# Two-layer trunk, first mixer: a fourth raw weight tile, memory's keys loaded behind head 0, Silus and exponentials pinned, the last output weights split first

## The chip, the cores and the metric

One Trainium2 chip; the kernel runs on one of its cores. The metric is the device time of one execution in microseconds (us), as the median of several runs. The engines are named as in the profile: PE (TensorE, matrix products; PEld are its weight loads), DVE (VectorE), ACT (ScalarE), POOL (GpSimd) and SP (SyncE, which issues most DMAs). POOL issues DMAs too. Each engine works through its own instructions in a fixed order; a letter q behind its name (SPq, POOLq) means its queue of issued DMAs and waits.

## The reference

An encoder trunk of two layers over 512 positions of width 1024, in float32. Each layer has a mixer and a gated channel mixer, both with a residual. The change lies in the first layer's mixer:

```python
h = rmsnorm(x, norm_mix_g[l])
proj = h @ a_w_in[a]
qk, v, o, gates, q_mem = jnp.split(proj, [...], axis=-1)
qk = jax.nn.silu(causal_dwconv(qk, a_conv_w[a], a_conv_b[a]))
q, k = jnp.split(qk, 2, axis=-1)
ig, fg = jnp.split(gates + a_gate_b[a], 2, axis=-1)
hm = mlstm_chunkwise(q, k, v, ig, log_sigmoid(fg))      # 4 heads of 192
hm = hm * lax.rsqrt(jnp.mean(hm * hm, axis=-1) + EPS) * a_head_g[a]
mix_out = hm * jax.nn.sigmoid(o)
mem_out = memory_attention(q_mem, mem, mem_w_kv[l])     # 4 heads of 64 over 256 tokens
x = x + jnp.concatenate([mix_out, mem_out], axis=-1) @ w_out
x = x + conv_ffn(rmsnorm(x, norm_ffn_g[l]), ...)
```

The second layer has a band attention of 12 heads in the place of the matrix memory (mLSTM), the same memory attention over its own keys and values, and the same form of output projection and channel mixer.

## The kernel before

**Products in three parts.** Activations stand as transposed tiles of 128 channels by 512 positions. Each float32 operand is split into a high part, rounded to the fp32r type (a cast on ACT, L130), and a low part, the difference (a subtraction on DVE, L131). A product is three matmuls: high by high, high by low, low by high (`mm3`, L169 to L171). A projection of 128 output channels (`project`) loads a weight tile of 128 x 1024 (`load`, L143, into a raw tile `wr`), splits it into `wh` and `wl` (`parts`), and runs eight `mm3`, 24 matmuls of 512 columns, into one PSUM bank.

**Pools.** Tiles with one tag share a fixed number of buffers (`bufs`): raw weights `wr` 3, their halves `wh` and `wl` 3 each, general tiles `u` 57, small tiles `s` 16, rows `bias` 4. An instruction that writes a tile waits until a buffer of its tag is free.

**The order of the instructions.** In the mixers a compile-time scheduler orders each engine's instructions: at each simulated moment it takes, of those that are ready, the one that was traced first. So the order in which the Python program traces is a priority, not a fixed order. `pin` (keep in program order) adds one edge: the instruction comes behind the one that was traced just before it on the same engine. The channel mixers' main loop has a fixed order written out by hand.

**The first mixer**, from about 60 to 262 us of the profile. `value_columns` makes the values; `gate_rows` turns the gates into rows `exponents` in DRAM and, at its end, columns `acol` and `floor2` (an Exp, L1099). `a_tiles` makes, for tile j, queries and keys (`qk_tile(j)`, `qk_tile(6 + j)`: projection, an Identity with the first conv tap on ACT (L1108), three taps on DVE (L1111), a Silu (L1112), then splits) and the output gate (`o_tile`, a Tanh, L1126). Tiles 3hp + 1 are shared by two heads: their halves go to masked tiles (`head_queries`, L499 to L503; `head_keys`, L509, L510).

A head (`mlstm_head`) goes through four steps s of 128 keys (`weighted_scores`): an Exp of a row of exponents (L1155), the issue of a later row's load, a causal mask on POOL (`affine_select`, L1157), the score matmuls into PSUM (`psc`), their product with the Exp on DVE (L1166), and a split into `pt` (L130, L131). The products with the values follow (`ptr`), then squares (L1193), statistics (L1200, L1201), a chain of small DVE instructions, a spread over the partitions (L244), and the split of the result into `mixes`. `spread_exponents` (L1029) loads a row of exponents, broadcast over the partitions, into a `bias` tile; `NEXT` (4) rows are loaded ahead, counted over all heads in order, so that the 16 rows are issued as the Exp four places before them is through.

`memory_attention` computes scores (L519), a softmax (L573 to L579, its Exps L576), transposes (L588), products (L602) and `values` (L538, L539). Its keys and values for both layers were computed at the start and spilled to DRAM; `load_memory_kv` (L523) loads them and splits them again (L509, L510, L130, L131).

`weave(job, filler, each)` advances the projections of the filler by a number of steps (one `mm3` each) for each step of a head or an attention. At the end the filler is the output projection: `OutProjection.part` adds up five of the eight output columns while heads are still at work, and `finish` computes the last three, adds the residual (L633), spills x (L634) and prepares the channel mixer's input. `finish` and `memory_attention` serve the second layer too, whose bands also use `bias` tiles.

The order of the stages around the change:

```python
weave(chain(value_columns(0), a_tiles(0, 1)), fill, 0.3)
run(fill)
fill = chain(a_tiles(2), a_memory_queries(0), a_tiles(3, 4), a_tiles(5), a_memory_queries(1))
memkv = load_memory_kv(0)
weave(mlstm_head(0), fill, 1.4)
until(lambda: og[2] is not None, fill)
weave(mlstm_head(1), fill, 1.125)
until(lambda: memq[0] is not None, fill)
weave(memory_attention(memq[0], memkv, 0, mixes), fill, 1.463, 4)
...
```

Of the kernel before, what the change touches and what calls it, by code (L numbers as in the profile page):

```python
# [12 lines left out]
AF = mybir.ActivationFunctionType  # L13
# [3 lines left out]
P = 128  # L17
D = 1024
S = 512
KT = D // P  # L20
TT = S // P
# [34 lines left out]
def trunk(  # L56
# [19 lines left out]
    V, A, G = nc.vector, nc.scalar, nc.gpsimd  # L76
# [2 lines left out]
    pool = ctx.enter_context(tc.tile_pool(name="pool", bufs=1))  # L79
    psum = ctx.enter_context(tc.tile_pool(name="psum", bufs=1, space=bass.MemoryType.PSUM))  # L80

    bufs = {"wr": 3, "wh": 3, "wl": 3, "u": 57, "t": 8, "pt": 2, "s": 16, "rb": 3, "bias": 4}
    pbufs = {"mm": 3, "sc": 3, "tr": 2}
    count = [0]
    dram = ctx.enter_context(tc.tile_pool(name="dram", bufs=1, space=bass.MemoryType.DRAM))
# [41 lines left out]
    pin = tc.keep_in_program_order  # L127
# [32 lines left out]
    def weights(*args):  # L160
        return parts(load(*args))

    def rows(w, c0, n, k0=0, k1=None):
        k1 = k1 if k1 is not None else w.shape[0] // P
        return w[k0 * P : k1 * P, c0 : c0 + n].rearrange("(k p) c -> p k c", p=P)
# [4 lines left out]
        nc.tensor.matmul(o, lh, rl, start=False, stop=False, skip_group_check=more)  # L170
        nc.tensor.matmul(o, ll, rh, start=False, stop=last, skip_group_check=more)  # L171

    def project(w, c0, act, tag="mm"):


        n = len(act)
        wh, wl = weights(rows(w, c0, P), n, P)
        o = ps(tag)
        for k in range(n):
            mm3(o, wh[:, k, :], wl[:, k, :], act[k][0], act[k][1], k == 0, k == n - 1)  # L180
            yield
        return o

    def run(gen):
        while True:
            try:
                next(gen)
            except StopIteration as end:
                return end.value

    def chain(*gens):
        for g in gens:
            yield from g
# [15 lines left out]
    def until(there, filler):  # L209
        while not there():  # L210
            next(filler)
# [35 lines left out]
    def logarithms():  # L247

        pin(A.preload_act_table_set("natural_log_exp_and_others"))
# [128 lines left out]
    ss = small(2 * TT).rearrange("p (c t) -> p c t", c=2)  # L378
# [43 lines left out]
    with tc.manual_schedule(engines={mybir.EngineType.PE, mybir.EngineType.Activation, mybir.EngineType.DVE}):  # L422

        w = ps("mm")
# [96 lines left out]
    def load_memory_kv(l):  # L521
        raw = sb("wr", [P, D])
        nc.sync.dma_start(raw, spill[l])  # L523
        k = head_keys(raw[:, :S])
        vs = []
        for m in range(2):
            v = sb("u", [P, S], F32R).rearrange("p (h c) -> p h c", h=4)
            src = raw[:, S + m * MEM : S + (m + 1) * MEM].rearrange("p (h c) -> p h c", h=4)
            split(v[:, :, :HD], v[:, :, HD:], src)
            vs.append(v)  # L530
        return k, vs
# [25 lines left out]
    def memory_attention(q, kv, hp, mixes):  # L557

        k, vs = kv
        pts = [sb("pt", [P, 5 * S], F32R) for _ in range(2)]  # L560
        pth = [p[:, : 2 * S].rearrange("p (a t) -> p a t", a=2) for p in pts]
        ptl = [p[:, 2 * S : 4 * S].rearrange("p (a t) -> p a t", a=2) for p in pts]
        es = {}

        def softmax(T2):
            ss = [ps("sc").rearrange("p (t m) -> p t m", t=2) for _ in range(2)]
            for i in range(2):
                T = 2 * T2 + i
                scores([s[:, i, :] for s in ss], q, slice(T * P, (T + 1) * P), k, slice(hp * MEM, (hp + 1) * MEM))
                yield  # L570
            for h in range(2):
                mx, sm = small(2), small(2)
                V.tensor_reduce(mx, ss[h], axis=AX.X, op=ALU.max, negate=True)  # L573
                e = sb("t", [P, S]).rearrange("p (t m) -> p t m", t=2)
                for i in range(2):
                    A.activation(e[:, i, :], ss[h][:, i, :], AF.Exp, bias=mx[:, i : i + 1], accum_out=sm[:, i : i + 1])  # L576
                V.reciprocal(sm, sm)
                for i in range(2):
                    V.tensor_scalar(e[:, i, :], e[:, i, :], sm[:, i : i + 1], None, op0=ALU.mult)  # L579
                es[T2, h] = e  # L580
                yield

        def transposed(T2):
            for h in range(2):
                tp = ps("tr").rearrange("p (a t c) -> p a t c", a=2, t=2)
                for i in range(2):
                    for a in range(2):
                        nc.tensor.transpose(tp[:, a, i, :], es[T2, h][:, i, a * P : (a + 1) * P], ident)  # L588
                tsl = slice(2 * T2 * P, 2 * (T2 + 1) * P)
                split(pth[h][:, :, tsl], ptl[h][:, :, tsl], tp.rearrange("p a t c -> p a (t c)"))  # L590
                yield

        yield from softmax(0)
        yield from softmax(1)
        yield from transposed(0)
        yield from transposed(1)
        outs = []
        for h in range(2):
            o2 = ps("tr")
            outs.append(o2)  # L600
            for i, (a, p) in enumerate(((0, pth), (0, ptl), (1, pth), (1, ptl))):
                nc.tensor.matmul(o2, vs[a][:, 2 * hp + h, :], p[h][:, a, :], start=i == 0, stop=i == 3)  # L602
            yield
        mixes[6 + hp] = values(outs)
        yield

    class OutProjection:
# [18 lines left out]

        def finish(self, gnames):
            logarithms()
            norm = Norm()
            acts = [[] for _ in gnames]  # L630
            for j in range(KT):
                o = self.o[j] if j in self.o else run(project(self.w, j * P, self.mixes))
                V.tensor_add(xT[j], xT[j], o)  # L633
                pin(G.dma_start(xspill[j], xT[j]))  # L634
                norm.add(xT[j])
                for a, g in zip(acts, gnames):
                    a.append(scaled(xT[j], g[:, j : j + 1]))
            return norm, acts
# [374 lines left out]
    tot = cpool.tile([AH, 16], F32, name="tot")  # L1013
    acol = cpool.tile([P, TT, AH], F32, name="acol")
    floor2 = cpool.tile([P, TT, AH], F32, name="floor2")
    NEXT = 4
    RO = [0, 512, 896, 1152, 1280]

    exponents = dram.tile([TT, AH, S], F32, name="exponents")
# [11 lines left out]
    def gate_rows():  # L1031
# [64 lines left out]
            nc.tensor.transpose(tp[:, T * AH : (T + 1) * AH], ar[:, T * P : (T + 1) * P], ident[:AH, :AH])  # L1096
            nc.tensor.transpose(tp[:, 16 + T * AH : 16 + (T + 1) * AH], mr[:, T * P : (T + 1) * P], ident[:AH, :AH])
        pin(V.tensor_copy(acol, tp[:, :16].rearrange("p (t h) -> p t h", t=TT)))
        A.activation(floor2, tp[:, 16:32].rearrange("p (t h) -> p t h", t=TT), AF.Exp, scale=-2.0)  # L1099

    mixes = [None] * KT

    def qk_tile(c):

        o = yield from project(w_in, c * P, act)
        acc = sb("t", [P, S])
        cw, cb = col["cw"], col["cb"]
        A.activation(acc, o, AF.Identity, scale=cw[:, 36 + c : 37 + c], bias=cb[:, c : c + 1])  # L1108
        for i in (1, 2, 3):
            w = cw[:, 12 * (3 - i) + c : 12 * (3 - i) + c + 1]  # L1110
            V.scalar_tensor_tensor(acc[:, i:], o[:, : S - i], w, acc[:, i:], op0=ALU.mult, op1=ALU.add)  # L1111
        A.activation(acc, acc, AF.Silu)  # L1112
        if c % 3 == 1:
            return (head_queries if c < 6 else head_keys)(acc)
        hi, lo = sb("u", [P, S], F32R), sb("u", [P, S], F32R)
        split(hi, lo, acc)
        return hi, lo
# [14 lines left out]
    def a_tiles(*js):  # L1132
        for j in js:
            qs[j] = yield from qk_tile(j)
            ks[j] = yield from qk_tile(6 + j)
        for j in js:
            og[j] = yield from o_tile(j)
# [3 lines left out]
    def a_memory_queries(hp):  # L1141
        memq[hp] = queries((yield from project(w_in, 4 * AW + 2 * AH + hp * P, act)), None)

    def mlstm_head(h):
# [6 lines left out]
        def weighted_scores(s):  # L1151
            n = S - s * P
            sl = slice(s * P, (s + 1) * P)
            e = sb("t", [P, S])
            A.activation(e[:, :n], spreads.pop((h, s)), AF.Exp, bias=acol[:, s, h : h + 1])  # L1155
            spread_exponents(order.index((h, s)) + NEXT)
            G.affine_select(  # L1157
                out=e[:, :P], in_=e[:, :P], pattern=[[1, P]], base=0, channel_multiplier=-1,
                compare_op=ALU.is_ge, fill=0.0,
            )  # L1160
            yield
            o = ps("sc")
            kf, qf = ks[full], qs[full]
            mm3(o[:, :n], kf[0][:, sl], kf[1][:, sl], qf[0][:, s * P :], qf[1][:, s * P :], True, False)
            head_scores(o[:, :n], odd, qs[sh], slice(s * P, S), ks[sh], sl, False, True)
            V.scalar_tensor_tensor(e[:, :n], o[:, :n], DH**-0.5, e[:, :n], op0=ALU.mult, op1=ALU.mult)  # L1166
            split(pt[:, RO[s] : RO[s + 1]], pt[:, 1280 + RO[s] : 1280 + RO[s + 1]], e[:, :n])
            yield
# [54 lines left out]
    fill = gate_rows()  # L1223
    weave(chain(value_columns(0), a_tiles(0, 1)), fill, 0.3)
    run(fill)
    fill = chain(a_tiles(2), a_memory_queries(0), a_tiles(3, 4), a_tiles(5), a_memory_queries(1))
    memkv = load_memory_kv(0)
    weave(mlstm_head(0), fill, 1.4)
    until(lambda: og[2] is not None, fill)
    weave(mlstm_head(1), fill, 1.125)  # L1230
    until(lambda: memq[0] is not None, fill)
    weave(memory_attention(memq[0], memkv, 0, mixes), fill, 1.463, 4)
# [290 lines left out]
```

## Time and profile before

| | |
|---|---|
| runs shown | 1194.70, 1194.93, 1196.32 us; median 1194.93 |
| the profiled execution | 1195.72 us; its span 1194.0 us |
| granted TensorE clock | 0.999 |
| instructions | 18184 |
| HBM | 128.89 MB read, 32.46 MB written, 135 GB/s over the span |

The span runs from the first to the last instruction of the profiled execution; times in the views are microseconds from its start. In a view of groups, the busy time, the mean duration of one instruction in ns and the idle time of the engine before them follow the name. In a timeline stand start, duration, engine, line, operation, tiles written and read, shape and count; in square brackets how long the engine was idle before, and what ended it. In the view of waits stand the waiting engine and tile, what released it, the sum in us, the count and the longest. Neighbouring instructions overlap by some tenths of a microsecond, since the ends are those of the pipeline; for TensorE the distance from start to start tells more than the busy time.

### The profile page before, as it was taken

To read this page: it belongs to the slowest core of one execution; us is meant where nothing else is said; L and a number is where in the kernel's file an instruction comes from. 1 tells how busy PE (TensorE), PEld (TensorE's weight loads), DVE (VectorE), ACT (ScalarE), POOL (GpSimd) and SP (SyncE) were. 2 spreads that over 40 slices of the span, in tenths; PEclk is the share of its full clock that TensorE was granted. 3 is DMA by queue.
4 is the path that set the end of the run, shared out by engine and by line. 5 is a ranking of instruction groups with operands and counts; after the bars stand their busy time and mean duration, and the time that the engine had idled before them with its cause. 6 is when DMAs were issued, how large, how long until landed. Compare 5 with 4: busy or idle time off the path is not lost.

```text
span 1194.0 us, 18184 instructions
## 1 busy us (share of the span) xinstructions
PE 1183.5 (99%) x6719; PEld 1037.0 (87%) x6719; DVE 961.7 (81%) x1760; ACT 725.2 (61%) x1294; POOL 130.3 (11%) x222
## 2 busy tenths in 40 slices
PE   9999999999999999999999999999999999999997
PEld 9988888888899998999888888888889988999986
DVE  6877788788978888888698888997896888888855
ACT  5648677655656555555576677776565655555545
POOL 1211201010021111111020000101001011011100
PEclk9999999999999999999999999999999999999999
DMA  8645313444265676665464313246336455665551
GB/s 289 212 108 140 84 54 80 152 144 141 88 156 147 156 165 165 154 144 123 142 204 123 89 54 101 69 135 185 111 99 141 116 139 135 142 141 139 119 158 71
DMA packets 200155, 158.61 MB, mean 133 GB/s; under 512 B 8344, under 2 KB 179838, under 8 KB 200066
## 3 DMA queue, kind: packets, MB, share of 16 engines
q1 hardware_dynamic: 183906, 119.74, 34.1%
q0 software_dynamic: 15584, 36.67, 14.9%
q8 instruction: 53, 0.87, 0.3%
q10 hardware_dynamic: 576, 1.05, 0.2%
q14 instruction: 36, 0.29, 0.1%
HBM read 128.89 MB, written 32.46 MB: 135 GB/s over the span
## 4 chain that ended last, share of the span: by engine, by line
PE 92%; ACT 3%; DVE 2%; DMA 1%; SPq 1%; issue 0%; POOL 0%; POOLq 0%; DVEq 0%; ACTq 0%
PE pmm L169 15%; PE pmm L170 15%; PE pmm L171 15%; PE ptr L171 6%; PE ptr L169 6%; PE ptr L170 6%; PE pmm L785 6%; PE psc L171 5%; PE psc L170 5%; PE psc L169 5%; PE pmm L784 3%; PE psc L519 2%; PE ptr L1350 1%; DMA wr<-in_mem_w_kv_dram 1%; PE ptr L1371 1%; PE ptr L1372 1%
## 5 line engine op out<-in xcount | busy, mean ns | idle before, releaser
L169 PE MATMUL pmm<-u,wh 128*128 128x512 f32 (+1 forms) x872 | 309.1, 355 | 0.3 <-ACT u L130 0.2
L170 PE MATMUL pmm<-u,wh 128*128 128x512 f32 (+1 forms) x872 | 306.2, 351 | 0.0
L171 PE MATMUL pmm<-u,wl 128*128 128x512 f32 (+1 forms) x872 | 306.0, 351 | 0.0
L131 DVE TENSOR_TENSOR wl<-wr,wh 128x1024 fp32r<-128x1024 f32 (+3 forms) x172 | 199.8, 1163 | 57.0 <-ACT wh L130 55.0
L130 ACT CAST wh<-wr 128x1024 fp32r<-128x1024 f32 (+3 forms) x172 | 172.4, 1004 | 97.7 <-PE pmm L170 44.5
L171 PEld LDWEIGHTS pmm<-u,wl 128*128 128x128 f32 x872 | 164.5, 189 | 21.1
L169 PEld LDWEIGHTS pmm<-u,wh 128*128 128x128 f32 x872 | 164.5, 189 | 18.5 <-ACT u L130 1.1
L170 PEld LDWEIGHTS pmm<-u,wh 128*128 128x128 f32 x872 | 164.7, 189 | 18.2 <-DVE u L131 0.5
L169 PE MATMUL ptr<-u,wh 128*128 128x512 f32 x272 | 106.7, 392 | 0.0
L171 PE MATMUL ptr<-u,wl 128*128 128x512 f32 x272 | 106.1, 390 | 0.0
L753 POOL DMA_DIRECT2D xspill<-t x64 | 55.6, 869 | 461.1 <-ACT t L752 450.4
L170 PE MATMUL ptr<-u,wh 128*128 128x512 f32 x272 | 105.9, 389 | 0.0
L130 ACT CAST u<-pt 128x512 fp32r<-128x512 f32 x102 | 63.0, 620 | 46.8 <-DVE pt L875 46.7
L131 DVE TENSOR_TENSOR u<-pt,u 128x512 fp32r<-128x512 f32 x102 | 69.9, 688 | 11.2 <-ACT u L130 8.5
L169 PE MATMUL psc<-u,wh 128*128 128x256 f32 (+1 forms) x232 | 76.1, 328 | 0.0
L171 PE MATMUL psc<-u,wl 128*128 128x256 f32 (+1 forms) x232 | 75.9, 327 | 0.0
L170 PE MATMUL psc<-u,wh 128*128 128x256 f32 (+1 forms) x232 | 75.9, 327 | 0.0
L937 ACT ACTIVATE t<-t 128x512 f32<-128x512 f32 x34 | 21.6, 634 | 79.3 <-DVE t L660 79.3
L785 PE MATMUL pmm<-u,u 128*128 128x512 f32 x192 | 69.6, 397 | 0.0
L821 DVE TENSOR_TENSOR t<-t,pmm 128x256 f32<-128x256 f32 x72 | 30.2, 419 | 44.9 <-ACT t L819 44.8
L752 ACT COPY t<-ptr 128x512 f32<-128x512 f32 x64 | 37.4, 585 | 43.1 <-PE ptr L171 43.1
L660 DVE SCALAR_TENSOR_TENSOR t<-t,cols,t 128x511 f32<-128x511 f32 x80 | 59.7, 746 | 3.7 <-ACT t L667 3.7
(300 smaller groups left out, 2673.8 us busy)
## 6 DMA issues: line engine op xcount, KB each, us to landing
wr<-in_ffn_w_up_dram SPq DMA_DIRECT2D x54, 512.0 KB, 4.2
wr<-in_ffn_w_down_dram SPq DMA_DIRECT2D x38, 512.0 KB, 4.1
pt<-in_ffn_w_up_dram SPq DMA_DIRECT2D x34, 512.0 KB, 6.2
xspill<-t POOLq DMA_DIRECT2D x64, 256.0 KB, 5.2
wr<-in_a_w_in_dram SPq DMA_DIRECT2D x20, 512.0 KB, 3.7
xspill<-u POOLq DMA_DIRECT2D x32, 256.0 KB, 2.6
u<-xspill SPq DMA_DIRECT2D x32, 256.0 KB, 5.0
wr<-in_w_kv_dram SPq DMA_DIRECT2D x12, 512.0 KB, 3.7
```

The source lines that it names most:

```text
L130: high = A.copy(hi, src) if on_act else V.tensor_copy(hi, src)
L131: low = V.tensor_tensor(out=lo, in0=src, in1=f(hi), op=ALU.subtract)
L169: nc.tensor.matmul(o, lh, rh, start=first, stop=False, skip_group_check=more)
L170: nc.tensor.matmul(o, lh, rl, start=False, stop=False, skip_group_check=more)
L171: nc.tensor.matmul(o, ll, rh, start=False, stop=last, skip_group_check=more)
L519: nc.tensor.matmul(o, a, b, start=first and i == 0, stop=i == 1)
L660: V.scalar_tensor_tensor(acc[:, n:], src[:, : S - n], self.fw[:, c * FT + j : c * FT + j + 1], acc[:, n:], op0=ALU.mult, op1=ALU.add,)
L752: A.copy(t, o)
L753: G.dma_start(xspill[j], t, accum_op=ALU.add)
L784: nc.tensor.matmul(r[:, :H], w[1][:, k], p[i - 1][:, :H], start=False, stop=False, skip_group_check=True)
L785: nc.tensor.matmul(r, w[0][:, k], p[i - 1], start=False, stop=k == n - 1, skip_group_check=True)
L821: V.tensor_tensor(out=o, in0=o, in1=r[:, H:], op=ALU.add)
```

## The change

Four parts of the first mixer change, and two of them are shared with the second. The raw weight tiles become four; for that, `bias` tiles go from 4 to 3, small tiles from 16 to 15, and 3 rows of exponents are loaded ahead instead of 4. `floor2` is copied out of PSUM by DVE in `gate_rows`, and its Exp stands, pinned, behind the two first groups of tiles. The Silus of `qk_tile`, the Exps of the heads and the Exps of the memory attentions (of both layers) are pinned. `load_memory_kv(0)` moves from before head 0 to after it. In `finish` (of both layers) the weights of the first two of the last three output columns are loaded and split before the residual additions are traced.

```diff
-    bufs = {"wr": 3, "wh": 3, "wl": 3, "u": 57, "t": 8, "pt": 2, "s": 16, "rb": 3, "bias": 4}
+    bufs = {"wr": 4, "wh": 3, "wl": 3, "u": 57, "t": 8, "pt": 2, "s": 15, "rb": 3, "bias": 3}
...
-    def project(w, c0, act, tag="mm"):
+    def project(w, c0, act, tag="mm", ready=None):
...
-        wh, wl = weights(rows(w, c0, P), n, P)
+        wh, wl = ready or weights(rows(w, c0, P), n, P)
...
                 for i in range(2):
-                    A.activation(e[:, i, :], ss[h][:, i, :], AF.Exp, bias=mx[:, i : i + 1], accum_out=sm[:, i : i + 1])
+                    pin(
+                        A.activation(
+                            e[:, i, :], ss[h][:, i, :], AF.Exp, bias=mx[:, i : i + 1], accum_out=sm[:, i : i + 1]
+                        )
+                    )
...
         def finish(self, gnames):
             logarithms()
+            rest = [j for j in range(KT) if j not in self.o]
+            ready = {j: weights(rows(self.w, j * P, P), KT, P) for j in rest[:2]}
             norm = Norm()
             acts = [[] for _ in gnames]
             for j in range(KT):
-                o = self.o[j] if j in self.o else run(project(self.w, j * P, self.mixes))
+                o = self.o[j] if j in self.o else run(project(self.w, j * P, self.mixes, ready=ready.get(j)))
...
-    NEXT = 4
+    NEXT = 3
...
-        A.activation(floor2, tp[:, 16:32].rearrange("p (t h) -> p t h", t=TT), AF.Exp, scale=-2.0)
+        V.tensor_copy(floor2, tp[:, 16:32].rearrange("p (t h) -> p t h", t=TT))
...
-        A.activation(acc, acc, AF.Silu)
+        pin(A.activation(acc, acc, AF.Silu))
...
-            A.activation(e[:, :n], spreads.pop((h, s)), AF.Exp, bias=acol[:, s, h : h + 1])
+            pin(A.activation(e[:, :n], spreads.pop((h, s)), AF.Exp, bias=acol[:, s, h : h + 1]))
             spread_exponents(order.index((h, s)) + NEXT)
...
     run(fill)
+    pin(A.activation(floor2, floor2, AF.Exp, scale=-2.0))
     fill = chain(a_tiles(2), a_memory_queries(0), a_tiles(3, 4), a_tiles(5), a_memory_queries(1))
-    memkv = load_memory_kv(0)
     weave(mlstm_head(0), fill, 1.4)
     until(lambda: og[2] is not None, fill)
+    memkv = load_memory_kv(0)
     weave(mlstm_head(1), fill, 1.125)
```

## The prediction

> **What bounds the kernel now.** I read the page's engine shares first, then the windows over the first mixer (60 to 262 us, the stage that most of the change touches), then the waits there, and last the timeline of the places where TensorE stood still.
>
> ```profile
> PE 1183.5 (99%) x6719; PEld 1037.0 (87%) x6719; DVE 961.7 (81%) x1760; ACT 725.2 (61%) x1294; POOL 130.3 (11%) x222
> 60.00:262.00 202.00, 201.52 (x1017) 170.36 (x1016) 155.34 (x314) 131.82 (x216) 22.93 (x48) 1.00 0.40 106
> 95.00:120.00 25.00, 25.00 (x122) 21.29 (x121) 17.86 (x27) 21.56 (x33) 3.55 (x8) 1.00 0.51 132
> 163.00:192.00 29.00, 28.92 (x142) 23.87 (x141) 23.79 (x43) 28.09 (x50) 2.10 (x4) 1.00 0.21 58
> 770.00:810.00 40.00, 39.36 (x217) 32.36 (x215) 35.39 (x99) 29.66 (x76) 1.30 (x2) 1.00 0.40 123
> ```
>
> After each stretch stand its length and the busy time of PE, PEld, DVE, ACT and POOL. TensorE (PE) is busy nearly all the time, at full granted clock (1.00). In the first mixer it lacks 0.48 us of 202. But the ends of matmuls are modelled, so I also measured from start to start. A 512-column matmul follows the one before after 0.23 us (186.43 to 186.66 below). These are the places where it took clearly longer:
>
> ```profile
> 186.43 0.39 PE L171 MATMUL pmm<-u,wl 128*128 128x512 f32 x1
> 186.66 0.39 PE L169 MATMUL pmm<-u,wh 128*128 128x512 f32 x1
> 187.12 0.73 PE L519 MATMUL psc<-u,u 128*128 128x512 f32 x2
> ...
> 233.04 0.28 PE L170 MATMUL psc<-u,u 128*128 128x128 f32 x1
> 233.47 0.73 PE L169 MATMUL ptr<-pt,u 128*128 128x512 f32 x2 [0.16 <-ACT pt L130]
> 234.04 0.22 PE L171 MATMUL psc<-u,u 128*128 128x128 f32 x1
> 234.35 0.50 PE L170 MATMUL ptr<-pt,u 128*128 128x512 f32 x1
> ...
> 251.75 0.39 PE L171 MATMUL ptr<-u,wl 128*128 128x512 f32 x1
> 252.30 0.96 PE L169 MATMUL pmm<-u,wh 128*128 128x512 f32 x3 [0.16 <-ACT u L130]
> ```
>
> Before 187.12 the step is 0.46 instead of 0.23: 0.23 lost, on head 2's shared keys. From 233.04 to 234.35 pass 1.31 us for two short matmuls (128 columns, a quarter of 0.23) and two long ones, 0.58 together: about 0.73 lost, on the first products of head 3 (`pt`). The step to 252.30 is 0.55: 0.32 lost, on head 3's mixes. That is **1.3 us in all**, nearly everything that this mixer can give. To be told from no change, a change must move about 0.2%, 2.4 us; less than that a measurement of this kernel can't tell.
>
> **The change part by part.**
>
> *The fourth raw tile* lets SyncE fetch one weight tile earlier. What do the splits wait for today?
>
> ```profile
> ACT wh L130 <- PE pmm L170: 11.8, 10, 3.8
> SPq L143 <- DVE wl L131: 181.0, 38, 12.4
> ```
>
> The first half of a split (ScalarE, `wh`) waits for TensorE to give a split buffer back, not for a DMA; the DMA queue waits for a free raw tile, up to 12.4 us, and its tiles are in time. An earlier load only lies longer: 0, neither gain nor loss.
>
> *Exponentials in program order.* A pin ties an instruction behind the one traced just before it on its engine. For a Silu that is the Identity of its own tile (L1108), on which it depends anyway: no effect. For a head's exponentials after the first it is mostly the cast of the step before (`pt`, L130): these run cast, Exp, cast, Exp from now on. floor2's Exp goes behind the Tanh of o tile 1, and head 0's first Exp behind that.
>
> ```profile
> L1112 ACT ACT_TABLE_LOAD x8 | 10.3, 1283 | 13.6 <-DVE t L1111 10.3 <-DVE s L1207 3.3
> L1155 ACT ACT_TABLE_LOAD x4 | 5.1, 1283 | 0.1
> L576 ACT ACT_TABLE_LOAD x3 | 3.8, 1283 | 0.1
> L1099 ACT ACT_TABLE_LOAD x1 | 1.3, 1283 | 0.0
> 106.75 0.58 ACT L1126 ACTIVATE u<-pmm 128x512 f32<-128x512 f32 x1
> 107.22 1.26 ACT L509 CAST u<-wr 64x512 fp32r<-64x512 f32 x2
> 108.50 0.72 ACT L130 CAST u<-wr 128x256 fp32r<-128x256 f32 x2
> 109.12 0.62 ACT L130 CAST pt<-t 128x512 fp32r<-128x512 f32 x1
> ```
>
> Sixteen loads of 1.283 us, for Silu and Exp in turn, stand in this mixer. With floor2 and head 0's first Exp behind the last Tanh (106.75) two pairs go: floor2's load and the Silu's after it, the first Exp's and the Silu's after that: 4 x 1.283 = 5.1 us of ScalarE. But there TensorE has no gap (25.00 of 25.00): worth 0. In exchange head 0's first cast comes later: the Tanh ends at 107.33, then load 1.28, Exp 0.73, issue and mask on POOL 0.86 and product 0.69 (rows of head 3 below): 110.9 instead of 109.12, 1.8 later. The two projections of tile 2, 48 matmuls of 0.23, 11 us, hide it; without them it would cost these 1.8. floor2's copy adds one tiny DVE instruction off every chain: 0.
>
> *Memory's keys behind head 0.* One load, four casts (1.26 + 0.72 us, rows above) and four subtractions move behind head 0. ScalarE waits there (3.75 us in the next row), and their reader is the memory attention, a whole head later. The load passes on SP's queue only weight loads that are early anyway. Head 1's first Exp is now queued behind the last of these casts, and its scores' product and cast wait for it. The 2 us fit into the 3.75: 0; with no such room, 2.0 later for head 1, under its filler.
>
> ```profile
> 128.25 0.63 ACT L1112 ACTIVATE t<-t 128x512 f32<-128x512 f32 x1 [3.75 <-DVE s L1206]
> ```
>
> *Three exponent rows ahead instead of four.* All four rows of a head were issued before it began; now row s3 is issued when the head's first Exp is through. On POOL that puts one DMA issue (0.57) between head 3's first Exp and its mask, where there was none; for the other heads one stood there already.
>
> ```profile
> 189.33 0.57 POOL L1029 DMA_DIRECT2D bias<-exponents  x1 [45.72 <-ACT t L1155]
> 230.53 0.73 ACT L1155 ACTIVATE t<-bias,acol 128x512 f32<-128x512 f32 x1
> 231.37 0.29 POOL L1157 TENSOR_SCALAR_AFFINE_SELECT t<-t 128x128 f32<-128x128 f32 x1 [33.49 <-ACT t L1155]
> 231.70 0.69 DVE L1166 SCALAR_TENSOR_TENSOR t<-psc,t 128x512 f32<-128x512 f32 x1 [0.36 <-POOL t L1157]
> 231.89 1.02 ACT L1155 ACTIVATE t<-bias,acol 128x384 f32<-128x384 f32 x2
> 232.82 0.60 ACT L130 CAST pt<-t 128x512 fp32r<-128x512 f32 x1
> 237.50 0.30 ACT L130 CAST pt<-t 128x128 fp32r<-128x128 f32 x1 [1.26 <-DVE t L1166]
> 239.45 0.22 PE L169 MATMUL ptr<-pt,u 128*128 128x128 f32 x1
> bias<-exponents POOLq DMA_DIRECT2D x4, 64.0 KB, 4.5
> DMA to landing us min/median/max: 2.9/3.6/7.7
> ```
>
> Here the sum is made. Today the product for s0 ends at 231.70 + 0.69 = 232.39, but two more exponentials hold ScalarE until 232.91, and the cast starts at 232.82. The pin alone would start it at 232.39: **-0.43**. The issue on POOL moves mask and product 0.57 later, to 232.96: together **+0.14** on the gap at 233.47. The steps after it are one chain now: Exp, mask, product, cast, four times. By the rows (an Exp 0.6 to 0.4, a mask 0.3, a product 0.56 to 0.28, a cast 0.5 to 0.3; the mixes' cast of about 0.6 once between), s1's cast ends near 236.1, s2's near 237.7 and s3's near 239.0; today s3's ends at 237.80 and TensorE uses it at 239.45. Row s3, issued from 231.26 on, lands at 235.8 to 236.4 by the median of 4.5, ahead of its Exp at 237.7. I estimate that the low half of s1 comes some 0.3 after TensorE asks for it: **+0.3**. Head 3's end has no slack (the gap at 252.30), so both are paid: **+0.4**. Bounds: -0.43, if only the pin counts; +1.5, if the cast of a weight tile, 1.05, falls into this chain as well.
>
> *Output weights split first.* Of the last three output columns two have their splits traced ahead of the residual additions now. But a free buffer is what they wait for:
>
> ```profile
> 252.27 1.05 ACT L130 CAST wh<-wr 128x1024 fp32r<-128x1024 f32 x1
> ```
>
> Column 5's cast already starts when the matmul of 251.75 has given its buffer back. From 252.30 ten steps of three matmuls (parts 4 and 5 of both groups), 6.9 us, stand before its use. No buffer comes free sooner by the new order: 0. The second split (1.05 on ScalarE, about as much on DVE) may run ahead of the additions that free PSUM; the 6.9 us hide that too, and without them it would be about 2.
>
> *The smaller pools reach the second mixer*: a band's second bias row is fetched when the band before reads its own for the last time. The rest of that band and its filler hide the landing: 0; without them 3.6, or 7.7 for the slowest landing shown.
>
> Sum: +0.4 on a span of 1194.0. That execution took 1195.72, 1.72 of it around the span, and 0.79 above the median of the runs, 1194.93. Against the median the forecast is **1195.3 us**.
>
> **The rivals.**
>
> *The table loads regroup* (faster, but little). From 163 us loads alternate Exp, Silu, Exp, Silu:
>
> ```profile
> 163.79 1.28 ACT L576 ACT_TABLE_LOAD   x1
> 165.66 1.28 ACT L1112 ACT_TABLE_LOAD   x1
> 166.96 0.63 ACT L1112 ACTIVATE t<-t 128x512 f32<-128x512 f32 x1
> 167.61 1.28 ACT L576 ACT_TABLE_LOAD   x1
> ```
>
> The Silu of 166.96 is traced ahead of all these exponentials. Taken first, two loads, 2.57 us, leave ScalarE's fullest stretch (28.09 of 29.00), and the 0.23 at 187.12 goes; with the pin's 0.43 and the POOL issue hidden, 1194.93 - 0.7 = 1194.2. Against it: the pin holds these Exps behind a weight cast that is done long before, not behind the Silu.
>
> *All stalls go*: 1.3 here, and in the second mixer 0.64 by the window from 770, perhaps 1.7 from start to start if it stands to the window as here (1.3 to 0.48): at most 1194.93 - 3.0 = 1191.9, and 1192.4 with most of them. Every chain would have to come earlier at once.
>
> *One more pair of table loads from 163 to 192 us* (slower). There TensorE already waits for ScalarE (the step to 187.12), so each microsecond more is paid. One more change of sets between the eight exponentials and the Silus costs 2 x 1.283 = 2.57; with the +0.4 that gives 1197.9. It decides as soon as a Silu is put between two exponentials once more than today; moved casts and later exponentials change what is ready when. Against it: program order holds only one Silu between them. The Trainium skill, page "ScalarE: Activation LUTs", section "What ACT_TABLE_LOAD costs", puts a switch of sets at about 2.66 us, the load and a drain of 1.38; by it the pair costs 5.3 and the time is an estimated 1200.6. The rows do not show that drain: the load of 165.66 is followed by its Silu 1.30 later.
>
> *Row s3 late*: landing after 7.7 puts it at 231.9 + 7.7 = 239.6, and Exp, mask, product, cast and low half (0.4 + 4 x 0.3) make 241.2, 1.75 after TensorE's use at 239.45: 1194.93 + 0.14 + 1.75 = 1196.8.
>
> **How the numbers follow.** Forecast (gaps shift, none of size made or closed) 0.46; regrouped loads 0.14; all stalls gone 0.08; row s3 late 0.12; one more pair of loads 0.20. Faster by over 0.2% is the third alone, 0.08; slower the last, 0.20; the rest, 0.72, is within. The range goes from 1193.0, below the regrouped case, to 1198.0, the extra pair; it leaves out the third case and whatever is worse than one pair.
>
> **What would show it.** Right: no load for floor2 near 90 us and 12 or 13 loads instead of 16; PE still 25.00 of 25 around head 0; a POOL issue ahead of head 3's first mask, and the gap at 233 still there. Wrong: a gap of 2 us or more near 187 with more loads before it; a PE wait that ends on a late exponent row; a new gap in the second mixer; or the gaps at 187, 233 and 252 all gone.

## The result, and the profile after

| | before | after |
|---|---|---|
| median of 4 runs, us | 1195.62 | 1210.70 (1210.12 to 1211.68) |
| the profiled execution | 1195.72, span 1194.0 | 1210.85, span 1209.1 |

The change makes the kernel slower: ratio 1.0129, 95% interval 1.0114 to 1.0144, 15 us. The forecast was 1195.3, in a range up to 1198.0.

The page and the windows of the changed kernel, in the columns of before. The first window here ends at 284 instead of 262, so the row of the kernel before for this window stands ahead:

```profile
60.00:284.00 224.00, 223.52 (x1114) 188.54 (x1113) 172.07 (x335) 143.85 (x233) 25.29 (x52) 1.00 0.42 113
```

```profile
PE 1198.8 (99%) x6719; PEld 1037.7 (86%) x6719; DVE 963.0 (80%) x1761; ACT 721.6 (60%) x1292; POOL 130.2 (11%) x222
60.00:284.00 224.00, 222.64 (x1077) 182.92 (x1077) 167.06 (x329) 136.88 (x224) 24.30 (x51) 0.99 0.40 110
95.00:120.00 25.00, 25.00 (x118) 20.91 (x117) 16.05 (x23) 16.77 (x27) 4.52 (x10) 1.00 0.37 90
```

PE has the same 6719 matmuls and is busy 15.3 us longer, with the same share of the span. In the stretch from 95 to 120 it is busy 25.00 of 25.00, as before; but the number in brackets has gone from 122 matmuls to 118. The place to read it cleanly is a stretch where nothing happens but matmuls of 512 columns: 290 to 320, in the first channel mixer, which no edit touches. The windows for PE alone (length, busy time and count, granted clock, DMA share, GB/s), before, then after:

```profile
290.00:320.00 30.00, 30.00 (x134) 1.00 0.29 88
```

```profile
290.00:320.00 30.00, 30.00 (x130) 1.00 0.30 88
```

Both are fully busy at full clock, and one does four matmuls fewer. From here on a *step* is the distance from the start of a matmul to the start of the next. Steps below 267 ns, that is those without a stall, with weights in `wh` or `wl` and 512 columns, average 228.43 ns before (2734 of them) and 232.44 ns after (2723). So every matmul of that kind takes 4 ns longer, in all stages: some 10.9 us.

Sorted by size, all steps of the run together give the 15.1 us of the span: +11.3 in steps less than 40 ns over the usual one of their shape, -0.3 in those of 40 to 100 ns over, and +4.1 in longer ones. Of the last, 1.7 are matmuls at half clock (below); the rest are waits in the first mixer. The largest is at head 1. First ACT, then PE, in the timeline:

```profile
136.72 1.21 ACT L130 CAST u<-u 128x512 fp32r<-128x512 f32 x2 [4.54 <-DVE u L1220]
137.84 1.26 ACT L509 CAST u<-wr 64x512 fp32r<-64x512 f32 x2
139.12 0.71 ACT L130 CAST u<-wr 128x256 fp32r<-128x256 f32 x2
139.85 1.28 ACT L1161 ACT_TABLE_LOAD   x1
141.15 0.72 ACT L1161 ACTIVATE t<-bias,acol 128x512 f32<-128x512 f32 x1
...
144.44 0.62 ACT L130 CAST pt<-t 128x512 fp32r<-128x512 f32 x1
```

```profile
144.03 0.22 PE L169 MATMUL psc<-u,u 128*128 128x128 f32 x1
144.09 0.27 PE L170 MATMUL psc<-u,u 128*128 128x128 f32 x1
144.21 0.28 PE L171 MATMUL psc<-u,u 128*128 128x128 f32 x1
144.32 0.27 PE L519 MATMUL psc<-u,u 128*128 128x128 f32 x1
145.11 0.73 PE L169 MATMUL ptr<-pt,u 128*128 128x512 f32 x2 [0.52 <-ACT pt L130]
```

ACT idles 4.54 us, casts head 0's mixes (`u<-u`), then memory's keys, and only then come the table load and head 1's first Exp (L1161, L1155 before). Its `pt` is cast at 144.44, and PE, whose last short product starts at 144.32, has nothing for another 0.69 us. Among the smaller ones, those at 196.60 (0.38), 205.65 and 206.07 (0.2 each) and 238.27 (0.48) stand ahead of products with `pt`. And one thing more, in the windows (all engines, then the clock):

```profile
249.60:253.00 3.40, 3.40 (x9) 2.65 (x9) 2.99 (x15) 0.00 (x0) 0.00 (x0) 0.50 0.36 99
253.00:256.40 3.40, 3.40 (x16) 2.75 (x16) 1.64 (x5) 0.47 (x1) 0.00 (x0) 1.00 0.20 60
```

For 3.41 us the granted clock is 0.50: nine matmuls in place of 16, which are the 1.7 us named above. The profile of before has no such window before its last microseconds.

The table loads of the first mixer, to be held against the sixteen of before:

```profile
L1118 ACT ACT_TABLE_LOAD x7 | 9.0, 1283 | 5.9 <-DVE t L1117 5.8
L577 ACT ACT_TABLE_LOAD x4 | 5.1, 1283 | 0.1
L1161 ACT ACT_TABLE_LOAD x2 | 2.6, 1283 | 0.0
L1232 ACT ACT_TABLE_LOAD x1 | 1.3, 1283 | 0.0
```

Four loads are gone around head 0, and two have come in the first memory attention: from 160 to 195 us there are seven, where before there were five (163.79 to 187.01). A second Silu now stands between its exponentials:

```profile
173.41 1.28 ACT L577 ACT_TABLE_LOAD   x1
175.29 1.28 ACT L1118 ACT_TABLE_LOAD   x1
177.24 1.28 ACT L577 ACT_TABLE_LOAD   x1
```

### The profile page after: what moved, and what is told of

Read it like the earlier page. It is cut to its first block, busy times and chain, and to the rows that moved or that the text cites. A ratio compares the mean times of both kernels' runs of the same rounds, so it can differ in the third digit from the quotient of the medians.

```text
span 1209.1 us, 18183 instructions
## 1 busy us (share of the span) xinstructions
PE 1198.8 (99%) x6719; PEld 1037.7 (86%) x6719; DVE 963.0 (80%) x1761; ACT 721.6 (60%) x1292; POOL 130.2 (11%) x222
## 4 chain that ended last, share of the span: by engine, by line
PE 95%; ACT 3%; DVE 1%; issue 0%; DMA 0%; SPq 0%; POOL 0%; ACTq 0%; DVEq 0%; POOLq 0%
PE pmm L169 15%; PE pmm L171 15%; PE pmm L170 15%; PE ptr L169 6%; PE ptr L170 6%; PE ptr L171 6%; PE pmm L791 6%; PE psc L170 5%; PE psc L169 5%; PE psc L171 5%; PE pmm L790 3%; PE psc L519 2%; PE ptr L1357 1%; PE ptr L1378 1%; PE ptr L1379 1%; PE ptr L592 1%
## 5 line engine op out<-in xcount | busy, mean ns | idle before, releaser
L131 DVE TENSOR_TENSOR wl<-wr,wh 128x1024 fp32r<-128x1024 f32 (+3 forms) x172 | 199.7, 1162 | 60.4 <-ACT wh L130 57.7
L170 PE MATMUL ptr<-u,wh 128*128 128x512 f32 x272 | 108.0, 397 | 0.0
L169 PE MATMUL ptr<-u,wh 128*128 128x512 f32 x272 | 108.0, 397 | 0.0
L131 DVE TENSOR_TENSOR u<-pt,u 128x512 fp32r<-128x512 f32 x102 | 69.9, 688 | 11.4 <-ACT u L130 8.5
```

Of the source, the lines that this page charges most:

```text
L131: low = V.tensor_tensor(out=lo, in0=src, in1=f(hi), op=ALU.subtract)
L169: nc.tensor.matmul(o, lh, rh, start=first, stop=False, skip_group_check=more)
```

## The experiments

Eighteen runs in four groups. A ratio is against runs of the kernel before on the same chip; the offset runs s17, s18, s24, wl_off, off64 and off32 are single times, read by their steps as well.

### Is it the pools, and which part of them?

The pools lie in SBUF one behind the other: `u`, `pt`, `wr`, `t`, `s`, `wh`, `wl`, `rb`, `bias`. All their tiles but the small ones are multiples of 2048 bytes per partition, so before the change all these pools start at the same place modulo 2048: the 16 small tiles of 128 bytes fill exactly 2048. With 15, `wh` and `wl` (and all behind them) stand 128 bytes lower against `u`; the fourth raw tile, 4096 bytes, changes nothing in that.

**s15**: before, with `"s": 15` alone.

> The kernel before with 15 small tiles instead of 16; every engine's order is the same as before, only the split weights (wh, wl) and what lies behind them in SBUF start 128 bytes lower, no longer at the same offset within 2048 bytes as the activations (u). Theory P (place in SBUF): the 512-column matmuls step by about 232 ns instead of 227, as in the profile after, and the time is about 1207 us (+11 to +12). Theory O (the new order of the instructions) and theory R (the fourth raw tile's earlier loads disturb TensorE): no difference, 1195.6 within 0.2%.

1205.38 us, ratio 1.0087 (1.007 to 1.0103): ten of the fifteen, with the order of every engine unchanged.

```profile
290.00:320.00 30.00, 30.00 (x131) 1.00 0.29 88
```

**pools_al**: all the new pool sizes and three rows ahead, no pin and no move; the small tile that is requested first is requested later, so that `s` comes to lie behind `wh` and `wl`, which then stand against `u` as before.

```diff
-    bufs = {"wr": 3, "wh": 3, "wl": 3, "u": 57, "t": 8, "pt": 2, "s": 16, "rb": 3, "bias": 4}
+    bufs = {"wr": 4, "wh": 3, "wl": 3, "u": 57, "t": 8, "pt": 2, "s": 15, "rb": 3, "bias": 3}
...
-    NEXT = 4
+    NEXT = 3
...
-    ss = small(2 * TT).rearrange("p (c t) -> p c t", c=2)
...
+        ss = small(2 * TT).rearrange("p (c t) -> p c t", c=2)
```

> The kernel before with the pools of the change alone (4 raw tiles, 3 bias tiles, 15 small tiles, 3 exponent rows ahead), wh and wl placed at u's offset as in the run before this one; no pin and no move. Theory P: 1195.6 to 1197 (at most the late exponent rows cost something). Theory R: 1207 or more with steps of 232 ns. Theory O: 1195.6.

1195.17, ratio 0.9999 (0.9989 to 1.0008). The fourth raw tile, the fewer small and `bias` tiles and the later rows are worth nothing either way. `rb` and `bias` stand 128 bytes off here and cost nothing.

**after_al**: the changed kernel with the same move of `ss`. **order**: before, with the changed order (all pins and moves) and the old pools and `NEXT`.

> The changed kernel with its 15 small tiles placed behind wh and wl in SBUF instead of ahead of them (one line moved; the order on every engine stays), so that wh and wl start at the same offset within 2048 bytes as u again. Theory P: the step is 227 ns again, 1199 us (the +3 to +4 of the waits remains). Theories O and R: 1210.7.

> All the reordering of the change (pins, memory's keys behind head 0, floor2's Exp, output weights first) with the pools and the 4 exponent rows ahead of the kernel before. Theory P: 512-column steps of 227 ns, and only the new waits in the first mixer remain: +3 to +4, 1199 us. Theory O: all of it, 1210.7. Theory R: 1195.6.

after_al 1201.93, ratio 1.0055 (1.0037 to 1.0072); order 1200.74, ratio 1.0048 (1.0033 to 1.0063). So the new order costs 5.7 by itself, more than the 3 to 4 that both expectations gave it, and the place of two pools the other nine or ten: 10.3 in s15, 8.8 between after and after_al, whose four runs spread from 1199.43 to 1204.10.

### What about the place?

**s17, s18, s24**: before, with `"s"` at 17, 18 and 24. **pad128, pad192**: before, with a constant of 128 or 192 bytes ahead of all large pools, which moves `u` and the weights together. **wl_off**: 128 unused bytes between `wh` and `wl`. **off32, off64**: small tiles of 160 bytes, 21 or 18 of them.

```diff
+    pad = cpool.tile([P, 32], F32, name="pad")      # pad128; 48 in pad192
+    V.memset(pad, 0.0)
...
-        return sb("s", [P, 32])[:, :n]
+        return sb("s", [P, 40])[:, :n]                # off32, off64
...
         hi = sb("wh", ...)
+        gap()                                         # wl_off: 128 bytes, once
         lo = sb("wl", ...)
```

> The kernel before with pool s at 17 tiles: the weight tiles wh and wl start 128 bytes later, at 192 instead of 64 bytes past a multiple of 2048; u stays at 64; every engine's order is unchanged. Theory P256 (the 512-column step is 227 ns when the weight tiles and u agree modulo 256 bytes, 232 ns otherwise): 192 against 64 disagree, 1205. Theory P2048 (they must agree modulo 2048): 1205 too. Theory LOW (only the shift downwards in the changed kernel hurts, for instance by a tile that crosses a boundary): 1195.

> Pool s at 18 tiles: the weight tiles start 256 bytes later, at 320 past a multiple of 2048, 64 past one of 256. P256: they agree with u modulo 256, so steps of 227 ns and 1195. P2048, and any rule that asks for agreement modulo 512 or 1024: steps of 232 ns and 1205.

> Pool s at 24 tiles: the weight tiles start 1024 bytes later, at 1088 past a multiple of 2048, 64 past one of 256, 512 and 1024. P256, and a rule modulo 512 or 1024: 227 ns and 1195. P2048: 232 ns and 1205.

> The kernel before with a constant of 128 bytes put ahead of all large pools: u, pt, t, wr, wh and wl all start at 192 past a multiple of 256, so they agree with each other, and none is where it was. One memset more at the start, nothing else. Theory REL (weights and moving tiles must agree modulo 256): steps of 227 ns, 1195. Theory ABS (it is the place of the weight tiles itself, 64 past a multiple of 256, that gives 227 ns): steps of 232 ns, 1205.

> The same with a constant of 192 bytes: all large pools start at a multiple of 256. REL: steps of 227 ns, 1195. ABS: either 232 ns and 1205, or, if a multiple of 256 is the best place, steps under 227 ns and less than 1190.

> The kernel before with one unused tile of 128 bytes between the pools wh and wl (one POOL memset more): wh and u stay at 64 past a multiple of 256, wl moves to 192. Of the three products of a block (wh by u's high part, wh by its low part, wl by its high part) only the third has its weights off. Theory W (a matmul is slowed while its own weight tile, or the one being loaded for the next, stands off the moving tile): a third of the 10.3, so 1198 to 1199, on one line in three. Rival B (both must agree, or the place of wh alone counts): 1195, or 1205.

> The kernel before with small tiles of 160 bytes, 18 of them: wh and wl stand 64 bytes off u modulo 256 (128 against 64); every engine's order is unchanged. Theory P256 (any disagreement modulo 256 costs): steps of 232 ns, 1205. Theory P128 is out, since 128 bytes off cost 10; theory GRADED: a part of it, 1198 to 1202. If 64 off happened to be a better place than 0: steps under 227 ns and under 1193.

> The same with 21 small tiles of 160 bytes: wh and wl stand 32 bytes off u modulo 256. P256: 1205. GRADED: less than the 64 bytes cost, 1196 to 1200.

Steps in ns are those of `u` by `wh` or `wl`, without stalls; the third column is how far these two stand behind `u` modulo 256.

| run | time, us | off, bytes | 512 columns | 256 columns |
|---|---|---|---|---|
| before | 1195.4 | 0 | 228.43 | 119.71 |
| s15 | 1205.38 | 128 | 232.32 | 119.02 |
| s17 | 1204.57 | 128 | 232.37 | 119.02 |
| s18 | 1196.67 | 0 (256 in all) | 228.46 | 119.71 |
| s24 | 1195.45 | 0 (1024 in all) | 228.45 | 119.71 |
| pad128 | 1194.94, ratio 0.9999 (0.9989 to 1.0008) | 0 | 228.48 | 119.71 |
| pad192 | 1195.05, ratio 0.9997 (0.9988 to 1.0007) | 0 | 228.49 | 119.71 |
| off32 | 1205.49 | 32 | 233.18 | 117.91 |
| off64 | 1201.38 | 64 | 233.30 | 115.50 |
| wl_off | 1203.10 | `wl` 128, `wh` 0 | 231.56 | 118.97 |

What counts is the distance between weights and moving tile, modulo 256, not where either stands: moved together, nothing changes. Any distance tried other than 0 costs the 512-column steps 4 to 5 ns, not less for 32 bytes than for 128, so GRADED falls; that off64's time lies in GRADED's range comes from its shorter 256-column steps. These behave otherwise: they get faster, most at 64 bytes, by 4.2 ns.

wl_off shows which matmul pays. Its timeline (lines are 11 higher there; L180 and L181 use `wh`, L182 `wl`):

```profile
300.17 0.39 PE L180 MATMUL pmm<-u,wh 128*128 128x512 f32 x1
300.39 0.40 PE L181 MATMUL pmm<-u,wh 128*128 128x512 f32 x1
300.63 0.40 PE L182 MATMUL pmm<-u,wl 128*128 128x512 f32 x1
300.86 0.39 PE L180 MATMUL pmm<-u,wh 128*128 128x512 f32 x1
```

0.22, 0.24, 0.23 in these rows; the medians over the run are 227, 232 and 234 ns. The third product uses `wl`, and during the second the weights of the third are being loaded. So it is two of three, 7.7 us by the time, where the expectation's sum counted one and came out at 1198 to 1199: in this one run a matmul is slow while weights that stand off are used or loaded. Modulo 256 is what the offsets tried agree on (32, 64 and 128 are slow, 256 and 1024 are not); why, no run shows.

### What in the order?

Runs with the old pools, in which the pin on the heads' Exps and the place of memory's keys are undone one by one; the rest of the new order stays in all four.

```diff
-            pin(A.activation(e[:, :n], spreads.pop((h, s)), AF.Exp, ...))       # o_nopin, o_both
+            A.activation(e[:, :n], spreads.pop((h, s)), AF.Exp, ...)
...
+    memkv = load_memory_kv(0)                                                   # o_keysback, o_both
     weave(mlstm_head(0), fill, 1.4)
     until(lambda: og[2] is not None, fill)
-    memkv = load_memory_kv(0)
```

> The run with the new order and the old pools (1200.7, +5.7 against before), with two parts of the order undone: the memory's keys are loaded ahead of head 0 again, and the heads' Exps of L155 are not pinned. Left of the change: floor2 as a copy with a pinned Exp, pinned Silus, the second mixer's pins, the output weights split first. Theory KC (the keys' casts behind head 0 together with the pinned Exps of the heads cost the +5.7): 1195 to 1196. Rival F (the other parts cost it): 1200.7 stays.

> The run with the new order and the old pools (1200.7), without the pin on the heads' Exps of L155; the memory's keys stay behind head 0. Theory K (the keys' casts on ACT behind head 0, with head 1's exponentials late behind them, cost the +5.7, whatever is pinned): 1199 to 1201. Theory C (the pins cost it, by holding Exps behind casts that are ready later): 1195 to 1197. Both share it: 1197 to 1199.

> The same run with the memory's keys ahead of head 0 again, and the pins kept. Theory K: 1195 to 1197. Theory C: 1199 to 1201. Both share it: 1197 to 1199.

| | keys ahead of head 0 | keys behind head 0 |
|---|---|---|
| Exps free | o_both 1196.31, 1.0009 (0.9999 to 1.0018) | o_nopin 1195.91, 1.0005 (0.9996 to 1.0015) |
| Exps pinned | o_keysback 1198.81, 1.0029 (1.0018 to 1.004) | order 1200.74, 1.0048 (1.0033 to 1.0063) |

Without the pin the keys cost nothing, and neither do the other pins, floor2 and the early output weights. With the pin and the keys ahead it is 2.5 over o_both; with the keys behind, 4.8 over o_nopin. The pin is the cause, the keys make it worse: theory C, with a share of K that exists only under the pin. The timelines of ACT around head 1, o_nopin, then order:

```profile
130.63 0.59 ACT L1132 ACTIVATE u<-pmm 128x512 f32<-128x512 f32 x1
131.24 1.28 ACT L1161 ACT_TABLE_LOAD   x1
132.53 0.72 ACT L1161 ACTIVATE t<-bias,acol 128x512 f32<-128x512 f32 x1
135.61 0.62 ACT L130 CAST u<-u 128x512 fp32r<-128x512 f32 x1 [2.36 <-DVE u L1220]
136.14 0.62 ACT L1161 ACTIVATE t<-bias,acol 128x384 f32<-128x384 f32 x1
...
139.47 1.03 ACT L130 CAST pt<-t 128x512 fp32r<-128x512 f32 x2
```

```profile
130.27 0.59 ACT L1132 ACTIVATE u<-pmm 128x512 f32<-128x512 f32 x1
135.28 1.22 ACT L130 CAST u<-u 128x512 fp32r<-128x512 f32 x2 [4.42 <-DVE u L1220]
136.40 1.26 ACT L509 CAST u<-wr 64x512 fp32r<-64x512 f32 x2
137.68 0.72 ACT L130 CAST u<-wr 128x256 fp32r<-128x256 f32 x2
138.42 1.28 ACT L1161 ACT_TABLE_LOAD   x1
139.71 0.73 ACT L1161 ACTIVATE t<-bias,acol 128x512 f32<-128x512 f32 x1
...
143.02 0.62 ACT L130 CAST pt<-t 128x512 fp32r<-128x512 f32 x1
143.54 0.62 ACT L1161 ACTIVATE t<-bias,acol 128x384 f32<-128x384 f32 x1
```

Free, the scheduler puts load and first Exp into ACT's idle time before head 0's last casts (131.24), and later Exps between other work; two steps' `pt` are cast together at 139.47. Pinned, the load waits behind head 0's casts, which wait for DVE, and behind the keys: the first Exp is 7.2 us later (132.53 against 139.71), the second one stands behind the first `pt` cast, and that cast is 3.5 us later. But most of these microseconds are hidden. PE stalls 0.64 at that place in o_nopin too, where `pt`'s low half (L131) comes late, against 0.79 in order (o_nopin, then order):

```profile
141.11 0.28 PE L171 MATMUL psc<-u,u 128*128 128x128 f32 x1
141.86 0.51 PE L170 MATMUL ptr<-pt,u 128*128 128x512 f32 x1 [0.47 <-DVE pt L131]
```

```profile
142.79 0.27 PE L519 MATMUL psc<-u,u 128*128 128x128 f32 x1
143.69 0.74 PE L169 MATMUL ptr<-pt,u 128*128 128x512 f32 x2 [0.62 <-ACT pt L130]
```

Added up stretch by stretch, what the steps of the two runs take over the usual one of their shape splits the 4.8 like this: 0.8 from 130 to 158 us (head 1), 0.5 from there to 175, 1.4 from 192 to 212 (head 2, where PE waits for `pt` at 196.57 and 205.42), 0.3 in head 3, and 1.7 in a half-clock window of 3.41 us at 153.56. The profiles of o_keysback, o_nopin and o_both have no such window before the end.

Against o_keysback, order loses the window's 1.7 and the same 1.4 in head 2, and gains 0.9 at other places; so what the keys add under the pin is not simply the 2 us of their casts. after, after_al and order, and none of the other profiles named in this part, have three things together: the stalls of head 2, the additional pair of table loads ahead of it, and a half-clock window. That the pair causes the stalls is likely, but no run has it alone, and what starts the window is open.

**after_fix**: the changed kernel as in after_al, without the pin on the heads' Exps; all other edits stay.

> The changed kernel with the two causes taken out: the small tiles behind wh and wl (as in the run after_al, 1201.9) and no pin on the heads' Exps of L155. All its other edits stay: four raw tiles, loads three ahead, the memory's keys behind head 0, floor2's copy and pinned Exp, pinned Silus, the second mixer's pins, the output weights first. Theory (place plus pins are the whole 15 us): 1195 to 1196.5. Rival (another edit still costs): 1198 or more; if an edit gains once the two are gone, under 1194.

1196.07, ratio 1.0005 (0.9996 to 1.0015). Place and pin are the whole loss, and beneath them the change gains nothing.

### A version that beats both

off64 had one shape slower and the other faster, so the place was chosen by shape. **best64**: before, with `wh` and `wl` tiles of 4352 bytes (17 x 256, so nothing else moves against `u`), in which the weights of the channel mixers' 256-column products begin at byte 64; **best192**: at byte 192.

```diff
-    def parts(raw, pinned=False):
+    def parts(raw, pinned=False, at=0):
...
-        hi = sb("wh", [P, D], F32R)[:, : a * b]...
+        hi = sb("wh", [P, D + 64], F32R)[:, at : at + a * b]...
...
-            self.a11, self.a12 = zip(*(self.halves(t) for t in parts(self.up)))
+            self.a11, self.a12 = zip(*(self.halves(t) for t in parts(self.up, at=16)))
...
-            self.s1, self.s3 = zip(*(self.halves(t) for t in parts(self.s13)))
+            self.s1, self.s3 = zip(*(self.halves(t) for t in parts(self.s13, at=16)))
```

> The kernel before with wh and wl tiles of 4352 bytes in place of 4096, so all stay at 64 past a multiple of 256; only the weights of the channel mixers' 256-column products (split_up and split_sums) begin 64 bytes into their tile. Order and work as before. In the run off64 the 1488 matmuls of 256 columns with weights in wh or wl fell from 119.7 to 115.2 ns a step, while the 512-column ones rose from 227 to 233. Theory (the best place depends on the columns: 0 for 512, 64 off for 256): about 1350 x 4.5 ns = 6.1 less, some 96 wide matmuls x 6 ns = 0.6 more, so 1189 to 1191. Rival (the time returns as waits for DVE and ACT, which set the pace of these stages): 1194 to 1196.

> The same with those weights beginning 192 bytes into their tile (64 bytes off on the other side, modulo 256). Theory SYM (only the distance counts): as with 64, 1189 to 1191. Rival (the side counts): 1193 to 1196.

best64 1190.17 us, ratio 0.9955 (0.9943 to 0.9968), over five runs; best192 1190.93, ratio 0.996 (0.9946 to 0.9974). Two stretches of 24 such matmuls, first and last rows, before and then best64:

```profile
408.18 0.28 PE L169 MATMUL pmm<-u,wh 128*128 128x256 f32 x1
...
410.95 0.28 PE L171 MATMUL pmm<-u,wl 128*128 128x256 f32 x1
```

```profile
407.17 0.28 PE L169 MATMUL pmm<-u,wh 128*128 128x256 f32 x1
...
409.79 0.28 PE L171 MATMUL pmm<-u,wl 128*128 128x256 f32 x1
```

2.77 us for 23 steps against 2.62: 120 ns a step against 114. Over the run the 256-column steps fall from 119.71 to 116.45 (1488 x 3.26 = 4.9 us), and the 512-column ones stay at 228.42. The other side (192) gives 116.72 and the same time within its interval, so SYM holds as far as it was tried. About a fifth of the expected 6.1 did not come: only some of these stretches go to 114, the others to 117.8, and what divides them is open.

## Why the prediction was wrong

**The step that failed first** is "The smaller pools reach the second mixer", costed at 0 with 3.6 or 7.7 as its price. It asked only when a band's row lands. That 15 small tiles in place of 16 move every pool behind them was no term of the sum, no bound and no rival. It is worth +10.3 (s15). No view of before shows it, since a place in SBUF has no row; but the pool sizes in the code do show that a whole set of matmul operands moves. What it moves is measured: 228.43 against 232.32 ns a step, with each engine's order the same.

**The second failed step is "Exponentials in program order".** Its mechanism was right: "one chain now: Exp, mask, product, cast, four times". Its size was not: +0.4, bounds -0.43 to +1.5, worked out for head 3 alone. Head 3 does cost 0.3 in order (0.9 in o_keysback); all heads together cost 2.5 with the keys ahead and 4.8 behind, 1.7 of the 4.8 in the half-clock window. The prediction looked for the pin's partner "for a head's exponentials after the first" and found it in the cast of the step before. For the first Exp of head 1 the partner is the last ACT instruction of head 0, or of the keys, and the Exp comes 7 us later, of which TensorE sees 0.8 from 130 to 158 us. What hid the chain in the forecast, the filler, hides all of it at head 0 and most of it at head 1, but leaves 1.4 in head 2.

**Memory's keys** were to fit into the 3.75 us of idle time before the Silu: 0, or 2.0 for head 1. They do not go there. In the changed kernel they run behind head 0's mixes, 137.84 to 139.83, in front of head 1's pinned Exp. That the Exp would be "queued behind the last of these casts" was said; that some of this is paid was not. Without the pin the 0 holds (o_nopin against o_both).

**Right at 0**, by pools_al and after_fix: the fourth raw tile, the rows three ahead, the Silus, floor2 and the output weights. Right too: head 0's first cast is later and hidden. That it stands at 110.78, forecast 110.9, is in part luck, since the slower matmuls have put off everything by then; in order it stands at 109.63. Also as forecast, floor2's load left its place near 90 (L1232, one load, at 106.74); the POOL issue comes ahead of head 3's mask:

```profile
235.85 0.56 POOL L1035 DMA_DIRECT2D bias<-exponents  x1 [32.16 <-ACT t L1161]
236.43 0.31 POOL L1163 TENSOR_SCALAR_AFFINE_SELECT t<-t 128x128 f32<-128x128 f32 x1
```

and the gap at 233 is still there, as 0.48 at 238.27. Of the loads, 12 or 13 were forecast; there are 14 (7 + 4 + 2 + 1). The two pairs around head 0 went as forecast, and one pair came in the first memory attention.

**The test "PE still 25.00 of 25"** came true and said nothing: 25.00 with 122 matmuls, 25.00 with 118.

**The rivals.** That pair is the event of the slowest rival, *one more pair of table loads*. What was held against it, "program order holds only one Silu between them", was wrong: there are two now. But it was not paid where it was priced, 2.57 at the gap of 187. That gap is gone, and from 175 to 192 us the steps take no more over their usual length than before (0.45 us against 0.49). If the pair is paid, it is in head 2, and not shown. So the rival's 1197.9 was on the right side with an event that happened, while the 15 us come for the most part from a term that it did not have. A regrouping that saves loads, a late exponent row and the closing of all stalls did not happen.

## What to carry to other kernels

A change of a pool's size moves the pools behind it: work out the place of each matmul's weights against its moving tile before and after, modulo 256 bytes here, and choose the place, whatever the small tiles in between do. In this kernel equal places were best for products of 512 columns, and 64 bytes off for those of 256. When busy time is full, read the count of instructions in the window, or the step from start to start; busy shares cannot show a matmul that became slower. And before pinning an instruction that a scheduler places freely, find what it will stand behind in each iteration, the first one above all, and what that waits for.

## What the runs showed of the hardware

- A 512-column float32 matmul's step grew from 228.4 to 232.3 ns with weights 128 bytes off the moving tile modulo 256, and to 233.2 with 32; a 256-column one's fell from 119.7 to 115.5 with 64. Other distances within 256 were tried only in best192 (192, for 256 columns: 116.7).
- Half-clock windows of 3.41 us appeared in the first mixer (after at 249.60, order at 153.56, after_al at 250.23) though no stall in the 12 us ahead of them was longer than 0.8 us. In all three, most or all of a head's statistics, 16 matmuls of two columns each, stand in the 3.4 us ahead; every run has these matmuls and most have no window, so this is a candidate and not a shown cause. The Trainium skill, page "TensorE: Matmul & The Clock Gate", section "Part 1: The HAM clock gate", puts the fall to half rate after an idle window of about 3.4 us; here PE is never idle that long, so by that rule they would not come. Their length agrees with that figure; what starts them is open.
